# First S5 layer of a four-layer trunk: a written transfer order with the small parameters ahead of x, and the turns and maps of three blocks moved in the instruction order

## Chip, cores and metric

The kernel runs on one core of one Trainium2 chip. The metric is the device time of one execution in microseconds (us), smaller is better. An execution of the kernel before takes 2290.04 us (median of 3 runs, 2288.98 to 2294.23).

The engines are named as the profile names them: PE (TensorE, matmuls), PEld (its weight loads), DVE (VectorE), ACT (ScalarE), POOL (GpSimd), SP (SyncE, which here only issues transfers). A "q" behind the name (SPq) is the engine's sequencer.

## The reference, cut to what matters

Four layers run over a sequence of 512 rows of width 1024, each a mixer and a feed-forward part. Layers 0 and 3 have an S5 mixer, layer 1 a gated linear attention, layer 2 a differential attention. The change is in the S5 mixer of layer 0, which for every group of 16 channels runs a diagonal complex recurrence with 64 states:

```
h = rmsnorm(x, norm_mix[layer])
dt = exp(log_dt)[:, None];  ab_mag = exp(lr * dt);  ab_ang = li * dt
bb = f * b                                # f from ab and lam
p_mag = exp(lr * dt * j);  p_ang = li * dt * j
s[t] = ab * s[t-1] + bb u[t]              # per group, complex
y = Re(c s) + d_skip * h
z = gelu(y);  a, b = split(z @ w_glu, 2);  mix = a * sigmoid(b)
```

## The kernel before

`s5_first` (L1596) computes the S5 mixer of layer 0. The kernel turns the complex recurrence into a real one by rotating with the angle of every state and step: a block of 128 state rows times 512 columns needs the cosine and sine of its angles (tile `cs`), the decay (`r4`), an input operator (`inm`), an output operator (`out`, four parts) and a direct operator, the map (`mop`, from the tile `rps`). Eight blocks, kk = 0 to 7, pass through a pipeline, `s5_pipe` (L1399), one step of its loop for each; operators of two blocks at a time come from the small parameters, in four groups of 8 channel pairs (h = kk // 2).

The steps of one block, with their lines:

- `up` (L1424, copy L1437): PE transposes the scaled input of the block, ACT copies it out.
- `products` (L1445, tile `V`): PE multiplies it with the input operator; the operator is X, made on DVE (L1131, L1106 to L1108), turned on PE (L1247, `xps`), copied by ACT (L1270).
- `states` (L1450 to L1455): six DVE operations multiply V with `cs`.
- `scan` (L1459) and `turn` (L1468, L1472): DVE runs the recurrence and turns the result back (`prods`).
- `outputs` (L1479, L1481, tile `y`): PE multiplies with the map and the output operator; ACT takes the gelu (L1483).
- `turned` (L1493 `zp`, L1494) and `rest` (L1497): PE transposes back, ACT and DVE split the result in a high and a low part.
- `glu` (L396 to L398): products with `w_glu`, whose tiles are split in two by ACT (L368) and DVE (L376).

The angles of a block come in four pieces, `s5_phases_first` (L1054): "rough" (two PE matmuls, L1066 and L1067, into a bank `rough`, then two ACT operations, L1068 and L1070, which round to whole turns, `turnsr`), "angle" (three PE matmuls, L1074 to L1076, of which L1075 subtracts `turnsr`), "clip" (DVE, L1079) and "sines" (ACT, L1082 to L1084). They need a row of frequencies, `frow`, which PE makes in two halves (L1049, copied by ACT at L1050): blocks 0 to 3 and blocks 4 to 7.

The map of a group, `s5_map` (L1216), takes `rps` (PE, L1213, `s5_rows`): DVE adds the skip term (L1223), ACT copies the rest (L1227), then the result goes through DRAM (L1229, L1238) into the map's place.

The small parameters are worked out in `s5_small` (L895): six small transfers (L916 to L923), four PE transposes (L930, L931, tile `s5ps`), then a chain of small DVE operations up to the parts of the frequency rows (L1044) and the first group's X. `loads()` (L1626), called in it behind the six, issues x (L1629, two transfers of 1 MB each), the norm's gain in pieces of 16 numbers (L1632, two transfers) and the raw b and c of the first two groups (L1116, L1119).

What sets the order: the order on an engine is the scheduler's own, except where `hand(...)` (L328) names an engine; from there to the next `hand` that engine's instructions stand as the code is written. In front of the first S5 layer `hand` names PE and ACT; `s5_pipe` then calls `hand_all` (all five engines). Inside the loop of `s5_pipe`, hooks written in `s5_first` (`first`, `behind_states`, `operators`, `ahead_of_zp`, `behind_products`, `behind_scans`, `beside`, `last`) say behind which step the angle pieces, maps and operators are written. An engine works through its instructions in that order: one that waits holds up all behind it.

Of the kernel before, what the change touches and what calls it, by code (L numbers as in the profile page):

```python
# [288 lines left out]
class Trunk:  # L289
# [1306 lines left out]
    def s5_first(self, ctx):  # L1596
# [5 lines left out]
        with self.tc.tile_pool(name="s5_0", bufs=1) as p:  # L1602
            scr, more = (self.hp.tile([P, 4096], F32, tag="hT", name=f"scr{z}") for z in range(2))
            oms = [more[:, 1024 * z : 1024 * z + 1024].rearrange("p (a b) -> p a b", a=2) for z in range(2)]
            mops = [more[:, 2048 + 1024 * z : 3072 + 1024 * z] for z in range(2)]
            bp = p.tile([P, 2, 256], F32, name="bpad")
            rs = p.tile([P, 2, 112], F32, name="rsb")
            self.rows_room = Slices(self.wp.tile([P, 2048], F32, tag="whl", name="params2", bufs=5))
            self.iota = self.rows_room.tile([P, P], I32, name="mi")
            nc.gpsimd.iota(self.iota[:], pattern=[[1, P]], base=0, channel_multiplier=0)  # L1610
            self.hand(mybir.EngineType.PE, mybir.EngineType.Activation)
            for z in range(2):
                self.zero_off(oms[z], 64, one=self.ones[:, :64])
            nc.vector.memset(rs[:, :, :48], 0.0)
# [23 lines left out]
            X, Q, ph, r4 = {}, {}, {}, {}  # L1638

            def new_x(h):  # L1640
                X[h] = self.s5_x(nc.vector, p, 0, 8 * h, 8, raw[h][0], 2, gain)
                X[h][1]()

            def new_q(h):
                Q[h] = self.s5_q(nc.vector, p, 0, 8 * h, 8, 2)
                Q[h][1](self.s5_qt(raw[h][1]))
# [30 lines left out]
            def phases(*pieces):  # L1677
                for kk, name in pieces:
                    if name == "rough":
                        ph[kk] = self.s5_phases_first(kk, cs(kk))  # L1680
                    ph[kk][name]()

            def decays(kk):
                r4[kk] = p.tile([P, 512], F32, tag="r4", name="r4", bufs=2)
                self.s5_decays(0, kk, r4[kk][:])

            def ins(kk):
                self.s5_inms(inm[kk % 2], self.s5_xts(X[kk // 2][0], 4 * (kk % 2)))

            def out_pads(kk):  # L1690
                self.s5_out_pads(oms[kk % 2], Q[kk // 2][0], slice(4 * (kk % 2), 4 * (kk % 2) + 4))
# [18 lines left out]
            def first(kk):  # L1710
                if kk == 2:
                    raw[3] = self.s5_loads(p, 0, 24, 8, 2)
                if 1 <= kk < 7:
                    decays(kk + 1)
                if kk == 2:
                    phases((5, "angle"), (6, "rough"))

            def behind_states(kk):
                if kk == 0:
                    new_x(1)  # L1720
                    X[1][2]()
                if kk == 1:
                    X[1][3]()
                    self.s5_b_pads(bp, X[1][0])
                if kk == 2:
                    phases((6, "angle"), (7, "rough"))

            def operators(kk):
                if kk == 1:
                    phases((3, "angle"), (4, "rough"))  # L1730
                if kk in (2, 4, 6):
                    h = kk // 2
                    self.s5_map(0, 8 * h, 8, self.s5_rows(8, bp, Q[h][0]), rs, mops[h % 2])
                if kk == 1:
                    new_q(1)
                if 1 <= kk < 7:
                    ins(kk + 1)
                if kk in (3, 5):
                    new_q(kk // 2 + 1)

            def ahead_of_zp(kk):
                if kk == 1:
                    phases((4, "angle"), (5, "rough"))
                if kk == 2:
                    phases((7, "angle"))

            def behind_products(kk):
                if kk == 0:
                    phases((2, "angle"))
                    rows[1]()  # L1750
                if kk == 3:
                    phases((5, "sines"), (6, "sines"), (7, "sines"))
                if kk % 2 == 0 and 2 <= kk < 7:
                    out_pads(kk + 1)
# [10 lines left out]
            def beside(kk):  # L1765
                h = kk // 2
                if kk == 0:
                    phases((2, "clip"), (2, "sines"), (3, "rough"))
                if kk == 1:
                    phases((4, "clip"), (3, "sines"), (4, "sines"))  # L1770
                if kk == 2:
                    phases((6, "clip"), (7, "clip"))
                if kk in (2, 4):
                    new_x(h + 1)
                    X[h + 1][2]()
                    X[h + 1][3]()
                    self.s5_b_pads(bp, X[h + 1][0])
                if kk % 2 and kk < 7:
                    Q[h + 1][2]()
                    Q[h + 1][3]()  # L1780
                    if kk > 1:
                        out_pads(kk + 1)

            def last(kk):
# [3 lines left out]
            rv = {}  # L1788
            hooks = {
                "first": first, "operators": operators, "behind states": behind_states, "ahead of zp": ahead_of_zp,  # L1790
                "behind products": behind_products, "behind scans": behind_scans, "beside": beside, "last": last, "late": (1,),
            }
            accs = self.s5_pipe(0, hu, zT, True, room, get, before, hooks)
# [743 lines left out]
```

## Time and profile before

| what | us |
|---|---|
| median of 3 runs (lowest, highest) | 2290.04 (2288.98, 2294.23) |
| the profiled execution's own time | 2288.5 |
| its span, first to last instruction | 2286.7 |
| PE busy | 2203.8 (96% of the span) |
| DVE busy | 1561.3 (68%) |
| ACT busy | 1120.9 (49%) |
| first S5 layer up to the last product of its second glu half | about 0 to 192 |

The profile is one execution, recorded instruction by instruction; all times in it are from the start of its span. 1.8 us of the execution lie outside the span. A row of the timeline has the start, the duration, the engine, the line, the operation and the tiles (out<-in), and in brackets the idle time of the engine before it with what ended that. A row of the chain of waits has start, time and what was on it. A row of the windows view has a stretch, its length, and each engine's busy time in it, then the clock granted to PE (1.00 is full), the busy share of the transfer engines and what they moved. "Queue" rows give the median time from a transfer's issue to its landing.

### The profile page before, as it was taken

How to read it: one execution, taken by the hardware profiler on the slowest of the kernel's cores; microseconds unless marked ns; L12 is line 12 of the kernel's file. 1: busy time of each engine (PE TensorE's matmuls, PEld its weight loads, DVE VectorE, ACT ScalarE, POOL GpSimd, SP SyncE). 2: the span in 40 equal slices, each digit the busy share in tenths (PEclk: the TensorE clock that was granted, in tenths of full speed). 3: DMA queues.
4: the chain of work that ended last, by engine and by line, in shares of the span. 5: the costliest groups of instructions: out<-in, count | busy, mean ns of one | idle time of the engine just before them, and what ended most of it. 6: DMA issues, size and time to landing. Idle time of an engine off the chain costs nothing.

```text
span 2286.7 us, 37220 instructions
## 1 busy us (share of the span) xinstructions
PE 2203.8 (96%) x14847; PEld 1957.1 (86%) x14847; DVE 1561.3 (68%) x2420; ACT 1120.9 (49%) x1870; POOL 281.3 (12%) x392
## 2 busy tenths in 40 slices
PE   4989999999999999999999999999999899999997
PEld 2778979898877799898988887999998788989996
DVE  7783887776624468777754675876766964957674
ACT  5534655454452366555545675744544234635352
POOL 1000141513000011101002131111000100101000
PEclk9899999999999999999999999999999999999999
DMA  3246666664322358666346466885641546767521
GB/s 83 41 113 188 146 170 177 159 177 118 113 75 77 121 135 204 179 172 175 88 139 133 94 147 163 225 217 140 175 101 39 153 142 157 185 165 175 155 77 65
DMA packets 295463, 317.83 MB, mean 139 GB/s; under 512 B 72221, under 2 KB 235353, under 8 KB 294906
## 3 DMA queue, kind: packets, MB, share of 16 engines
q1 hardware_dynamic: 233050, 234.23, 34.0%
q0 software_dynamic: 62240, 81.22, 19.1%
q8 instruction: 117, 1.92, 0.3%
q14 instruction: 56, 0.46, 0.1%
HBM read 283.54 MB, written 16.65 MB: 131 GB/s over the span
## 4 chain that ended last, share of the span: by engine, by line
PE 82%; DVE 8%; ACT 4%; issue 3%; DMA 2%; SPq 1%; POOL 0%; ACTq 0%; DVEq 0%; POOLq 0%
PE a L565 18%; PE acc L396 14%; PE acc L398 13%; PE acc L397 13%; PE c L565 8%; PE d L565 4%; PE y L1481 2%; DVE whl L376 2%; ACT whl L368 1%; PE s L2302 1%; PE V L1445 1%; PE op L2336 1%; PE tp L123 1%; PE y L1479 1%; DVE halves L229 1%
## 5 line engine op out<-in xcount | busy, mean ns | idle before, releaser
L376 DVE TENSOR_TENSOR whl<-wst,whl 128x1024 fp32r<-128x1024 f32 x272 | 331.5, 1224 | 258.0 <-ACT whl L368 257.3
L368 ACT CAST whl<-wst 128x1024 fp32r<-128x1024 f32 x272 | 283.8, 1050 | 307.5 <-PE acc L398 225.3
L565 PE MATMUL a<-side,whl 128*128 128x256 f32 x3168 | 382.5, 277 | 4.0 <-DVE whl L376 3.6
L565 PEld LDWEIGHTS a<-side,whl 128*128 128x128 f32 x3168 | 369.2, 188 | 6.8 <-DVE whl L376 5.4
L396 PE MATMUL acc<-whl,act 128*128 128x512 f32 x704 | 278.4, 396 | 1.7 <-DVE x L548 1.7
L397 PE MATMUL acc<-whl,act 128*128 128x512 f32 x704 | 274.7, 390 | 0.0
L398 PE MATMUL acc<-whl,act 128*128 128x512 f32 x704 | 274.7, 390 | 0.0
L565 PE MATMUL c<-side,whl 128*128 128x256 f32 x2112 | 254.3, 277 | 1.2 <-DVE whl L376 1.2
L565 PEld LDWEIGHTS c<-side,whl 128*128 128x128 f32 x2112 | 246.7, 188 | 2.0 <-DVE whl L376 2.0
L376 DVE TENSOR_TENSOR whl<-slot,whl 128x1024 fp32r<-128x1024 f32 x107 | 130.5, 1223 | 70.0 <-ACT whl L368 70.0
L396 PEld LDWEIGHTS acc<-whl,act 128*128 128x128 f32 x704 | 132.1, 188 | 32.1 <-issue 2.7
L398 PEld LDWEIGHTS acc<-whl,act 128*128 128x128 f32 x704 | 132.2, 188 | 28.1
L397 PEld LDWEIGHTS acc<-whl,act 128*128 128x128 f32 x704 | 132.2, 188 | 25.5
L368 ACT CAST whl<-slot 128x1024 fp32r<-128x1024 f32 x107 | 112.1, 1053 | 82.7 <-PE acc L398 34.9
L396 PE MATMUL acc<-whl,hT 128*128 128x512 f32 x352 | 142.5, 405 | 0.0
L398 PE MATMUL acc<-whl,hT 128*128 128x512 f32 x352 | 137.9, 392 | 0.0
L397 PE MATMUL acc<-whl,hT 128*128 128x512 f32 x352 | 137.8, 391 | 0.0
L565 PE MATMUL a<-sides,whl 128*128 128x256 f32 x1056 | 134.5, 283 | 0.0
L565 PEld LDWEIGHTS a<-sides,whl 128*128 128x128 f32 x1056 | 129.7, 191 | 1.2
L565 PE MATMUL d<-sides,whl 128*128 128x256 f32 x1056 | 126.5, 276 | 1.0 <-ACT whl L368 1.0
L565 PEld LDWEIGHTS d<-sides,whl 128*128 128x128 f32 x1056 | 122.8, 188 | 1.2 <-ACT whl L368 1.2
L704 ACT CAST act<-r 128x512 fp32r<-128x512 f32 (+1 forms) x110 | 66.3, 646 | 115.0 <-DVE r L683 107.8
(458 smaller groups left out, 3879.2 us busy)
## 6 DMA issues: line engine op xcount, KB each, us to landing
wst<-in_ffn_w_gate_up_dram SPq DMA_DIRECT2D x88, 512.0 KB, 4.7
wst<-in_ffn_w_down_dram SPq DMA_DIRECT2D x88, 512.0 KB, 4.3
slot<-in_ffn_w_gate_up_dram SPq DMA_DIRECT2D x71, 512.0 KB, 5.8
wst<-in_ffn_w_gate_up_dram POOLq DMA_DIRECT2D x44, 512.0 KB, 6.2
halves<-in_ffn_w_gate_up_dram SPq DMA_DIRECT2D x43, 512.0 KB, 5.0
wst<-in_s_w_glu_dram SPq DMA_DIRECT2D x32, 512.0 KB, 4.5
wst<-in_gla_w_in_dram SPq DMA_DIRECT2D x24, 512.0 KB, 3.6
wst<-in_diff_w_qkv_dram SPq DMA_DIRECT2D x24, 512.0 KB, 4.2
```

What stands on the lines that cost most here:

```text
L123: tr.nc.tensor.transpose(p[:, j], h[:, j * P : (j + 1) * P], tr.ident[:])
L229: v.tensor_tensor(s, s, y, op=op)
L368: self.last["high"] = self.nc.scalar.copy(hl[:, 0], w[:])
L376: self.last["low"] = self.nc.vector.tensor_tensor(hl[:, 1], w[:], hl[:, 0].bitcast(F32), op=ALU.subtract)
L396: mm(out, lh, rh, start=first, stop=False)
L397: mm(out, lh, rl, start=False, stop=False)
L398: self.last["mm"] = mm(out, ll, rh, start=False, stop=last)
L565: mm(o, hl[:, x, k, c], side[y][:, k], start=first and not (j or k or n), stop=k == 3 and n == 2, skip_group_check=True,)
L704: self.last["act high"] = nc.scalar.copy(dst[:, 0, j], src[:, j])
L1445: mm(V[kk][z][:, bs(b)], inm[:, z, bs(b)], U[:, bs(b)], start=True, stop=True)
L1479: mm(yb[:, b], U[:, bs(b)], mop[:, bs(b)], start=True, stop=False)
L1481: mm(yb[:, b], q[:, j, b], om[:, j // 2, bs(b)], start=False, stop=j == 3)
```

## The change

Three edits, all in `s5_first`; no operation is added or taken away.

1. `hand` names SP too, in front of the small parameters. SP's transfers then stand as written: the six small ones first, x and the gain behind them.
2. The rough turns of the fourth block (kk = 3) are written behind the angle of the third in `behind_products(0)`, ahead of the second half of the frequency rows, where they stood in `beside(0)` behind the sines of block 2.
3. The third step (kk = 2): the map of the second group (`rps` and what takes it) is written in `behind_states`, ahead of block 1's outputs, where it stood in `operators`, behind them; the angle pieces of blocks 5, 6 and 7 each move one or two hooks later.

```
-            self.hand(mybir.EngineType.PE, mybir.EngineType.Activation)
+            self.hand(mybir.EngineType.PE, mybir.EngineType.Activation, mybir.EngineType.SP)
...
             def first(kk):
...
-                if kk == 2:
-                    phases((5, "angle"), (6, "rough"))
+
+            def maps(kk):
+                h = kk // 2
+                self.s5_map(0, 8 * h, 8, self.s5_rows(8, bp, Q[h][0]), rs, mops[h % 2])
...
             def behind_states(kk):
...
                 if kk == 2:
-                    phases((6, "angle"), (7, "rough"))
+                    maps(2)
+                    phases((5, "angle"), (6, "rough"))
...
             def operators(kk):
...
-                if kk in (2, 4, 6):
-                    h = kk // 2
-                    self.s5_map(0, 8 * h, 8, self.s5_rows(8, bp, Q[h][0]), rs, mops[h % 2])
+                if kk in (4, 6):
+                    maps(kk)
...
             def ahead_of_zp(kk):
...
                 if kk == 2:
-                    phases((7, "angle"))
+                    phases((6, "angle"), (7, "rough"))
...
             def behind_products(kk):
                 if kk == 0:
-                    phases((2, "angle"))
+                    phases((2, "angle"), (3, "rough"))
                     rows[1]()
+                if kk == 2:
+                    phases((7, "angle"))
...
             def beside(kk):
...
                 if kk == 0:
-                    phases((2, "clip"), (2, "sines"), (3, "rough"))
+                    phases((2, "clip"), (2, "sines"))
```

How the instructions stand. On SP, from its first transfer on, the kernel before has x (`xin`) and one half of the gain at the head:

```order
L1629 DMA xin<-in_x_dram 128x2048 x2
L1632 DMA gain<-in_norm_mix_dram 64x32x16
L916 DMA params<-in_s_lam_re_dram 64x128
L917 DMA params<-in_s_lam_im_dram 64x128
L919 DMA params<-in_s_log_dt_dram 64x2
L921 DMA params<-in_s_d_dram 16x128
L922 DMA params<-in_norm_mix_dram 8x128
L923 DMA params<-in_norm_ffn_dram 32x128
L1632 DMA gain<-in_norm_mix_dram 64x32x16
L1116 DMA bb<-in_s_b_re_dram 128x8x16
```

The changed kernel, from the same place:

```order
L916 DMA params<-in_s_lam_re_dram 64x128
L917 DMA params<-in_s_lam_im_dram 64x128
L919 DMA params<-in_s_log_dt_dram 64x2
L921 DMA params<-in_s_d_dram 16x128
L922 DMA params<-in_norm_mix_dram 8x128
L923 DMA params<-in_norm_ffn_dram 32x128
L1629 DMA xin<-in_x_dram 128x2048 x2
L1632 DMA gain<-in_norm_mix_dram 64x32x16 x2
L1116 DMA bb<-in_s_b_re_dram 128x8x16
```

The six small transfers have gone past x and the first half of the gain; both halves of the gain now follow each other. Everything behind is in the old order.

On ACT, in the first step of the loop, behind the copy of block 2's input (- is before, + is the changed kernel; `frow` is the second half of the frequency rows, `rsb` the first group's map):

```order
 L1437 COPY room_352<-up 128x512
+L1068 ACTIVATE turns<-rough,magic 128x512
+L1070 ACTIVATE turnsr<-turns,mmagic 128x512
 L1050 CAST frow<-frow 12x512
 L1227 COPY rsb<-rps 128x2x48
```

The two roundings of block 3 stood behind six sine operations (L1082 to L1084, blocks 1 and 2) and now stand ahead of them.

On PE, in the third step, behind the transposes of block 0's result (`zp`), the first rows of the piece that moved (up to the first outputs of block 1):

```order
 L1481 MATMUL y<-scr_97,prods 128x128 x4
 L1493 MATMUL zp<-ident,gain 128x128 x4
-L1074 MATMUL angle<-counts,frow 128x512
-L1075 MATMUL angle<-turnsr,nident 128x512
-L1076 MATMUL angle<-counts,frow 128x512
-L1066 MATMUL rough<-counts,frow 128x512
-L1067 MATMUL rough<-counts,frow 128x512
+L1213 MATMUL rps<-Q,bpad 32x64 x16
 L1074 MATMUL angle<-counts,frow 128x512
 L1075 MATMUL angle<-turnsr,nident 128x512
```

The map's matmuls (`rps`) now stand right behind `zp`; they stood behind the eight rows of block 1's outputs. Block 5's angle stands behind them, block 6's angle behind block 4's `up`, block 7's rough behind that, and block 7's angle behind block 3's products. DVE's order is the same in both kernels.

## Prediction

> **What bounds it now.** I read the chain of waits first, then the timeline of the first 157 us by engine, then the windows view, to see what an earlier S5 layer is worth at the end of the kernel.
>
> The chain's head (start, time, what):
>
> ```profile
> 2.50 5.78 SPq L916
> 8.33 0.60 SPq L917
> 8.97 0.60 SPq L919
> 9.61 0.58 SPq L921
> 10.23 0.37 SPq L922
> 10.65 1.67 DMA params<-in_norm_ffn_dram
> ...
> 12.75 0.49 DVE params L940 x3
> ```
>
> The kernel begins with a queue. The issue of the first small parameter takes 5.78 us, behind the two transfers of x and one of the gain; five more issues follow, the last lands 1.67 us after its issue, and only at 12.75 us can DVE start on the parameters. From there to 27.38 us the chain is DVE's small operations, then PE's frequency rows.
>
> The windows view (length, busy PE, PEld, DVE, ACT, POOL with counts, granted PE clock, transfer share, GB/s):
>
> ```profile
> 51.73:61.97 10.24, 6.83 (x56) 5.18 (x56) 10.21 (x17) 6.76 (x14) 0.10 (x1) 0.50 0.44 88
> 72.21:75.62 3.41, 1.90 (x6) 0.95 (x6) 1.92 (x2) 2.96 (x5) 0.10 (x1) 1.00 0.62 87
> 75.62:82.45 6.83, 6.83 (x28) 6.02 (x28) 0.00 (x0) 1.41 (x2) 0.00 (x0) 0.50 0.09 21
> 91.88:156.57 64.69, 56.78 (x571) 50.77 (x569) 64.21 (x110) 25.28 (x46) 0.31 (x3) 0.97 0.30 64
> 157.00:192.00 35.00, 34.33 (x174) 28.69 (x174) 12.58 (x12) 12.88 (x16) 0.86 (x1) 1.00 0.61 203
> 192.00:2286.70 2094.70, 2056.40 (x13651) 1834.80 (x13649) 1418.60 (x2106) 1029.70 (x1719) 270.59 (x358) 0.99 0.55 143
> ```
>
> From 91.88 to 156.57 DVE is the bound (64.21 of 64.69 us busy); from 157 to the end PE is (34.33 of 35, then 2056.40 of 2094.70). Nothing behind the layer waits for a clock time: its weights are loaded as buffers come free. So every microsecond by which DVE reaches the stretch from 91.88 earlier should come through to the end. The two places that the change touches in the loop lie just ahead, and there PE ran at half clock (0.50) for 10.24 and 6.83 us.
>
> **Edit 1, the transfer order.** Without the queue in front, lam_re's issue should take what its neighbour of the same size, lam_im (L917), takes: 0.60 us, with a step to the next of 0.64 (8.33 to 8.97). The last small one is then issued at 0.81 (SP's first issue) + 3 × 0.64 + 0.62 + 0.42 = 3.77 us instead of 10.65: **6.9 us earlier**. DVE would start at about 5.9. The rows that bear on its cover (the timeline's, and L971 from the chain):
>
> ```profile
> 0.81 0.87 SPq L1629 DMA_DIRECT2D xin<-in_x_dram  x2
> 8.80 1.13 ACT L1386 ACTIVATE scr<-xin,rs 128x1024 f32<-128x1024 f32 x1
> 19.11 0.26 ACT L891 ACTIVATE params<-params 128x64 f32<-128x64 f32 x1 [9.18 <-DVE params L887]
> 21.39 0.27 DVE pw L971
> 25.86 0.42 DVE L1131 TENSOR_TENSOR bb<-bb,gain 128x256 f32<-128x256 f32 x1
> 27.38 1.02 PE L1049 MATMUL frow<-ident,params 128*12 128x128 f32 x4 [14.66 <-DVE params L1044]
> ```
>
> What pays for it is x, which goes out right behind, at about 4.1 instead of 0.81: 3.3 us later. ACT scales the first part of x ahead of the two sines of the parameters, up to 8.80 + 1.13 = 9.9 here, so up to 13.2 at the latest. The first sine would like to start at 19.11 − 6.9 = 12.2; a microsecond late, the two end some 0.7 us behind that, at 13.9, and DVE takes them (L971) at 21.39 − 6.9 = 14.5. Covered, with 0.6 us to spare. DVE and PE have nothing else to do at 5.9.
>
> The other cover is thinner. The gain's second half now stands right behind the first and takes over the stall, and the raw b behind it is wanted at 25.86 − 6.9 = 19.0 (a row of the timeline, and one of the transfers by line, with the median us to landing at its end):
>
> ```profile
> 11.68 1.26 SPq L1116 DMA_DIRECT2D bb<-in_s_b_re_dram  x1
> bb<-in_s_b_im_dram SPq DMA_DIRECT2D x3, 64.0 KB, 2.9
> ```
>
> The stall ended at 2.50 + 5.78 = 8.3, 7.5 us after x's first issue, so now at 11.6. Then comes 1.3 for b's real part, which here took the delay that the second gain makes, and its imaginary part lands 2.9 after its own issue: 15.8, or 17.1 if the second gain costs as much again. That leaves 2 to 3 us of slack; a stall twice as long (5.8 more) would cost DVE 2.6 to 3.9. I take −6.9, with ends −3 and −6.9.
>
> **Edit 2, block 3's turns.** Rows of the timeline:
>
> ```profile
> 54.37 0.72 ACT L1070 ACTIVATE turnsr<-turns,mmagic 128x512 fp32r<-128x512 f32 x1
> 55.14 0.80 PE L1075 MATMUL angle<-turnsr,nident 128*128 128x512 f32 x1 [6.49 <-ACT turnsr L1070]
> 56.39 0.56 DVE L1108 TENSOR_TENSOR X<-X,dx 128x384 f32<-128x384 f32 x1
> 59.34 1.97 PE L1247 MATMUL xps<-ident,X 64*64 64x64 f32 x32
> 63.55 0.69 DVE L1079 TENSOR_SCALAR cs<-angle 128x512 f32<-128x512 f32 x1 [1.39 <-PE angle L1076]
> ```
>
> PE waits 6.49 us for a rounding that ACT does behind six sines. Moved ahead of them it is done five to six us earlier, and that wait goes. But PE's next work but one, the turn of X (`xps`), needs DVE's X, ready at 56.95. In old times it can start at 57.0 instead of 59.34: **2.3 us**, not 6.5; the rest of the wait moves to `xps`. Queued behind `xps` are block 3's `up`, block 4's angle, block 2's products and block 0's outputs, all of which move with it. DVE itself gains only the 1.39 us of its wait at L1079. The price: two roundings of some 0.7 us each stand ahead of the frequency rows, the first map's copy and block 1's sines on ACT, so these come up to 1.4 us later; the sines are wanted by DVE's states of block 1, five operations further on, so I cost it at nothing, and at 0.5 if that cover is short.
>
> The clock moves this term. PE's work from L1075 to `xps` took 59.34 − 55.14 = 4.2 us at half clock; begun some 5.5 us sooner, it ends by about 53.8, and PE is idle for 3 us until 57.0. So a half-clock stretch will be there, shorter or a window longer. `xps` at full clock (1.15 in the next part's rows, against 1.97 here) would make it −3.1; one more 3.41 us stretch at half speed costs 1.7 us of PE and leaves −0.6. I take −2.0.
>
> **Edit 3, the second group's map.**
>
> ```profile
> 71.70 0.50 PE L1074 MATMUL angle<-counts,frow 12*128 12x512 f32 x1
> 73.35 0.39 PE L1074 MATMUL angle<-counts,frow 12*128 12x512 f32 x1
> 73.37 1.23 DVE L376 TENSOR_TENSOR whl<-wst,whl 128x1024 fp32r<-128x1024 f32 x1 [0.25 <-ACT whl L368]
> 75.25 0.50 PE L1075 MATMUL angle<-turnsr,nident 128*128 128x512 f32 x1 [1.51 <-ACT turnsr L1070]
> 77.25 0.80 PE L1479 MATMUL y<-scr,room 128*128 128x128 f32 x2
> 84.38 0.69 PE L1213 MATMUL rps<-Q,bpad 128*32 128x64 f32 x32
> 85.13 1.15 PE L1247 MATMUL xps<-ident,X 64*64 64x64 f32 x32
> 85.17 0.37 DVE L1223 SCALAR_TENSOR_TENSOR rsb<-mask,dcol,rps 128x16 f32<-128x16 f32 x2 [10.58 <-PE rps L1213]
> 90.28 0.48 PE L396 MATMUL acc<-whl,zT 128*128 128x512 f32 x1
> 90.68 1.29 DVE L1079 TENSOR_SCALAR cs<-angle 128x512 f32<-128x512 f32 x2
> ```
>
> This is the longest wait of the layer: DVE stands 10.58 us in front of the map's skip term, and scan, turns and all behind it stand too. Now `rps` follows `zp` and takes 0.75 (84.38 to 85.13), from 71.70 to 72.5, so DVE can go on at 74.6, as soon as L376 ends. Not all of 10.6 us is won, since block 7's angle has gone back behind block 3's products, and DVE's clip of it (the second of the two at 90.68, so 91.3) stands ahead of the next X. PE's way there: `rps` 0.75; block 1's outputs; `xps`, `up`, one angle, `zp` and block 3's products, which ran from 85.13 to 90.28, 5.15; and besides two angles and one rough, of which an angle with a rough took 1.65 (71.70 to 73.35) and an angle alone some 1.2. With the outputs as here, mostly at half clock (77.25 to 84.38, 7.1 us), the sum is 71.70 + 0.75 + 7.13 + 5.15 + 1.65 + 1.2 = 87.6: **−3.7**. At the full clock of block 0's outputs (rows below, 65.80 to 70.46, 4.7 us) it is 85.2: **−6.1**.
>
> ```profile
> 65.80 0.39 PE L1479 MATMUL y<-scr,room 128*128 128x128 f32 x2
> 70.46 0.60 ACT L1483 ACTIVATE gain<-y 128x512 f32<-128x512 f32 x1
> ```
>
> Behind the clip everything is DVE's: X, block 3's states, and its gapless stretch. Does the clock stay up? In the kernel before it fell behind the stretch from 72.21 to 75.62, in which PE was busy 1.90 of 3.41 us, with the 1.51 us wait at L1075 in it. `rps` now fills part of that gap, and block 6's rounding is no longer waited for there. I give it even odds and take the middle, −4.9.
>
> The Trainium skill (TensorE: Matmul & The Clock Gate, section "What's actually happening") says that the clock halves after at least one idle window of about 3.4 us and returns after one busy window. By that rule half-idle windows do no harm, block 1's outputs run at full clock, edit 3 gives its far end, and the whole change 1.2 us more than my sum. The trace disagrees: a window busy 56% was followed by two at half clock, the first of them fully busy.
>
> **Sum.** −6.9 − 2.0 − 4.9 = **−13.8 us**. The profiled execution (2288.5: 2286.7 of span and 1.8 around it) would become 2274.7. The median of the runs shown is 1.5 us above that execution, so I predict **2276.2**. All ends together give −3 − 0.6 + 0.5 − 3.7 = −6.8 and −6.9 − 3.1 − 6.1 = −16.1.
>
> **Rivals.**
>
> *Only the head counts.* PE, idle ahead of `xps`, stays at half clock from there to block 7's angle: the other 9 us of that way (5.15 + 1.65 + 1.2 + 0.75) double too, DVE waits at both clips, and what edits 2 and 3 give is gone. For it: half clock followed both waits of before, and PE has a new one at `xps`. Against: the longest half-clock stretch here was 10.24 us, and it ended while PE was busy. Time: 2290.0 − 6.9 = 2283.1.
>
> *x or b comes late.* The pieces of gain and b are queued behind x, and if the stall doubles, DVE stands at L1131 for up to 3.9 us. For it: the trace shows the stall's size once. Against: the transfer behind the second gain took only 1.26. Time: 2290.0 − 13.8 + 3.9 = 2280.1.
>
> *The small parameters gain nothing.* If the first small transfer is slow whatever stands in front of it, the head stays. Against: x's two issues, the first of all, took 0.87 together. Time: 2290.0 − 2.0 − 4.9 = 2283.1.
>
> *Slower: the clock never comes back.* PE runs DVE's stretch from 91.88 to 156.57 at half clock as well, since DVE-fed work leaves gaps in every window. There PE has 7.9 us of room (64.69 − 56.78), and each 3.41 us stretch at half speed takes 1.7 of it. The first five cost nothing; from about thirteen on the 13.8 us are gone, and with all nineteen the time is 2290.0 − 13.8 + 19 × 1.7 − 7.9 = 2300.6. Against: PE's clock there is 0.97 now, with the same gaps.
>
> **How the numbers follow.** A difference of 0.2% (4.6 us) is about what a measurement of this kernel can tell from no change. Forecast (−9 to −17): 0.72. Only the head: 0.12. x or b late: 0.08, still faster by over 0.2%. Head gains nothing: 0.05, of which I put 0.03 within 0.2%. Slower: 0.03, of which 0.02 beyond 0.2%. Faster by over 0.2%: 0.92, leaving some of the "only the head" cases inside the bound; within: 0.06; slower: 0.02. The range goes from 2271.5 (the far ends, 2290.0 − 16.1 = 2273.9, less 2.4 for the spread of runs, 2288.98 to 2294.23) to 2283.5, which takes in the first three rivals at their own times.
>
> **What would show it.** In the changed kernel's profile: lam_re's issue under 1 us, the stall at a gain transfer, DVE's L940 near 5.9 and PE's L1049 near 20.5. PE's wait at L1075 for block 3's turns gone, and one of 2 to 5 us at `xps` ended by DVE's X. DVE's wait at L1223 gone, and two short ones at L1079 ended by PE's angle. The stretch of DVE at full load starting near 78. I would be wrong if DVE's L1131 waits for a transfer, or if PEclk shows more than five half-clock stretches between 45 and 90 us.

## The result, and the profile after

| | changed kernel | kernel before |
|---|---|---|
| median of 7 runs each, us | 2281.15 (2275.9 to 2285.19) | 2291.11 (2288.98 to 2294.44) |
| the profiled execution's own time | 2281.29 | 2288.5 |
| its span | 2279.4 | 2286.7 |

The ratio is 0.9953, with a 95% interval from 0.9939 to 0.9967: 10.8 us off 2291, between 7.6 and 14.0. The prediction was 13.8 off, 2276.2, with a range from 2271.5 to 2283.5. The two profiled executions are only 7.3 us apart in span; that of before is 2.6 us below its median, that of after at its median.

The head first: the changed kernel's timeline of SP.

```profile
0.81 0.57 SPq L916 DMA_DIRECT2D params<-in_s_lam_re_dram  x1
...
5.04 6.68 SPq L1632 DMA_DIRECT2D gain<-in_norm_mix_dram  x2
```

lam_re's issue, 5.78 us before, takes 0.57; the stall has moved to the gain's two (6.68 together, of which the second took 5.97). Next, DVE's timeline of the changed kernel, from the first parameters to the last clip.

```profile
5.94 0.49 DVE L940 COPY params<-s5ps 128x64 f32<-128x64 f32 x3 [1.63 <-PE s5ps L931]
...
14.79 0.27 DVE L971 TENSOR_TENSOR pw<-params 128x64 f32<-128x64 f32 x1
...
32.73 0.69 DVE L1450 TENSOR_TENSOR mods<-V,cs 128x512 f32<-128x512 f32 x1 [0.64 <-ACT cs L1084]
...
47.17 0.69 DVE L1450 TENSOR_TENSOR mods<-V,cs 128x512 f32<-128x512 f32 x1 [1.19 <-ACT cs L1084]
...
68.33 1.23 DVE L376 TENSOR_TENSOR whl<-wst,whl 128x1024 fp32r<-128x1024 f32 x1 [0.25 <-ACT whl L368]
69.47 0.37 DVE L1223 SCALAR_TENSOR_TENSOR rsb<-mask,dcol,rps 128x16 f32<-128x16 f32 x2
...
76.74 0.69 DVE L1079 TENSOR_SCALAR cs<-angle 128x512 f32<-128x512 f32 x1 [1.68 <-PE angle L1076]
80.85 0.69 DVE L1079 TENSOR_SCALAR cs<-angle 128x512 f32<-128x512 f32 x1 [3.42 <-PE angle L1076]
...
87.03 0.68 DVE L1450 TENSOR_TENSOR mods<-V,cs 128x512 f32<-128x512 f32 x1
```

The same places in DVE's timeline of the kernel before (those that the prediction did not show):

```profile
38.58 0.69 DVE L1450 TENSOR_TENSOR mods<-V,cs 128x512 f32<-128x512 f32 x1 [0.65 <-ACT cs L1084]
...
51.74 0.69 DVE L1450 TENSOR_TENSOR mods<-V,cs 128x512 f32<-128x512 f32 x1
...
97.47 0.68 DVE L1450 TENSOR_TENSOR mods<-V,cs 128x512 f32<-128x512 f32 x1
```

Read the shift down the layer. L940 is 6.8 us earlier (5.94 against 12.75), block 0's states 5.9 (32.73 against 38.58), block 1's 4.6 (47.17 against 51.74), L376 5.0 (68.33 against 73.37), and behind the map and the clips block 3's states 10.4 (87.03 against 97.47). So the head arrives in full and is partly lost by block 1; edit 2 adds nothing that can be seen; edit 3 adds 5.4. The wait of 10.58 us at L1223 is gone and two others, 1.68 and 3.42, stand at L1079. Now PE's timeline of the changed kernel:

```profile
20.79 1.02 PE L1049 MATMUL frow<-ident,params 128*12 128x128 f32 x4 [14.89 <-DVE params L1044]
...
29.91 3.52 PE L1445 MATMUL V<-room,inm 128*128 128x128 f32 x16
...
44.78 0.50 PE L1075 MATMUL angle<-turnsr,nident 128*128 128x512 f32 x1 [0.57 <-ACT turnsr L1070]
...
52.44 1.12 PE L1247 MATMUL xps<-ident,X 64*64 64x64 f32 x16 [3.82 <-DVE X L1108]
...
113.67 0.46 PE L1479 MATMUL y<-scr,room 128*128 128x128 f32 x2 [2.21 <-DMA scr<-rd]
```

L1049 is 6.6 us earlier, L1075 waits 0.57 instead of 6.49, and a wait of 3.82 us for DVE's X stands at `xps`. Two things are not in the prediction. V of block 0 took 3.52 us; before it took 2.05, since PE was back at full clock by then. And the first y of block 5 waits 2.21 us for the map that comes out of DRAM; behind it DVE waits 1.48 us for PE at its last L1223. The chain of waits of the changed kernel runs through that trip:

```profile
105.15 1.83 DMA rd<-rsb
107.38 1.75 SPq L1238
111.54 1.89 DMA scr<-rd
```

Behind 110 us the shift shrinks from 10.4 to 8.0 (the first L376 behind the last scan at 151.17 instead of 159.17). In a second profile of the kernel before that L376 stands at 160.24, so rows this far down are good to about 1 us. That leaves three questions: what took part of the head's gain, what edit 2 is worth, and what the map's trip costs.

### The profile page after: what moved, and what is told of

The parts are those of the page before. It is cut to its first block, busy times and chain, and to the rows that moved or that the text cites. A ratio compares the mean times of both kernels' runs of the same rounds, so it can differ in the third digit from the quotient of the medians.

```text
span 2279.4 us, 37223 instructions
## 1 busy us (share of the span) xinstructions
PE 2204.5 (97%) x14847; PEld 1956.4 (86%) x14847; DVE 1560.5 (68%) x2420; ACT 1120.6 (49%) x1870; POOL 281.6 (12%) x392
## 4 chain that ended last, share of the span: by engine, by line
PE 81%; DVE 9%; ACT 4%; issue 2%; DMA 2%; SPq 1%; POOL 0%; ACTq 0%; DVEq 0%; POOLq 0%
PE a L565 17%; PE acc L396 14%; PE acc L398 13%; PE acc L397 13%; PE c L565 8%; PE d L565 4%; PE y L1481 2%; DVE whl L376 2%; ACT whl L368 1%; PE V L1445 1%; PE s L2306 1%; PE op L2340 1%; PE tp L123 1%; DMA wst<-in_ffn_w_gate_up_dram 1%; DVE halves L229 1%
## 5 line engine op out<-in xcount | busy, mean ns | idle before, releaser
L376 DVE TENSOR_TENSOR whl<-wst,whl 128x1024 fp32r<-128x1024 f32 x272 | 331.6, 1224 | 260.2 <-ACT whl L368 259.4
L376 DVE TENSOR_TENSOR whl<-slot,whl 128x1024 fp32r<-128x1024 f32 x107 | 130.5, 1223 | 70.2 <-ACT whl L368 70.2
```

The costliest lines, as they stand in the source:

```text
L376: self.last["low"] = self.nc.vector.tensor_tensor(hl[:, 1], w[:], hl[:, 0].bitcast(F32), op=ALU.subtract)
```

## The experiments

Each kernel ran beside the kernel before on the same chip; a ratio is to that kernel, with its 95% interval. By these intervals the difference of two rows of the table is uncertain by some 4 us. In the table, us saved is (1 − ratio) × 2291; "block 1" is the start of block 1's L1450 in the profile. "52 products" and the like are extra PE products whose result nobody reads; their place is given with the run.

| run | median us | ratio | us saved | block 1 |
|---|---|---|---|---|
| edit 1 | 2284.95 | 0.9971 [0.9958, 0.9984] | 6.6 | 47.70 |
| edits 1, 2 | 2284.34 | 0.9973 [0.9962, 0.9984] | 6.2 | 48.64 |
| edits 1, 3 | 2279.48 | 0.9956 [0.9944, 0.9969] | 10.1 | 47.43 |
| changed kernel (1, 2, 3) | 2281.15 | 0.9953 [0.9939, 0.9967] | 10.8 | 47.17 |
| 1, 2, 3 + 100 products | 2287.02 | 0.9978 [0.9967, 0.9988] | 5.0 | 52.07 |
| 1, 2, 3 + 52 products | 2277.69 | 0.9936 [0.9923, 0.9949] | 14.7 | 44.91 |
| 1, 3 + 52 products | 2275.42 | 0.9929 [0.9916, 0.9943] | 16.3 | 45.22 |
| before + 52 products | 2288.93 | 0.9994 [0.9984, 1.0003] | 1.4 | 52.10 |
| 1, 2, 3 + 52 + 10 products | 2278.88 | 0.9941 [0.9929, 0.9952] | 13.5 | 45.25 |
| 1, 2, 3, map on two queues | 2278.61 | 0.9939 [0.9926, 0.9951] | 14.0 | 47.33 |
| 1, 2, 3 + 52 + 10, two queues | 2276.07 | 0.9924 [0.9913, 0.9936] | 17.4 | 45.28 |
| the same, turns one step later | 2275.32 | 0.9931 [0.9916, 0.9945] | 15.8 | 43.82 |

### Edit 1 alone

```diff
-            self.hand(mybir.EngineType.PE, mybir.EngineType.Activation)
+            self.hand(mybir.EngineType.PE, mybir.EngineType.Activation, mybir.EngineType.SP)
```

> Edit 1 alone. Theory (each edit is paid at its own place, the turns cost about what they give, the map gives 5 and loses 2.4 of it later): PE's frequency rows L1049 at 20.8 as in the changed kernel, DVE's states of block 0 (L1450) 6 to 6.6 us earlier than before, less where the clock's turn to full falls late; DVE's wait of about 10.6 us at L1223 is back; time 2291.1 less 6 = 2285 (2283.5 to 2287). Rival 'only the head counts': as fast as the changed kernel, 2281 to 2283. The prediction's own sum would have it at 2284.2, with 6.9 of the 13.8.

Measured: 2284.95, 6.6 us saved (3.7 to 9.6), beside 6.9 in the prediction's sum. DVE's timeline of this run:

```profile
47.70 0.69 DVE L1450 TENSOR_TENSOR mods<-V,cs 128x512 f32<-128x512 f32 x1 [1.66 <-ACT cs L1084]
...
68.60 1.23 DVE L376 TENSOR_TENSOR whl<-wst,whl 128x1024 fp32r<-128x1024 f32 x1 [0.25 <-ACT whl L368]
...
80.27 0.37 DVE L1223 SCALAR_TENSOR_TENSOR rsb<-mask,dcol,rps 128x16 f32<-128x16 f32 x2 [10.44 <-PE rps L1213]
...
92.55 0.68 DVE L1450 TENSOR_TENSOR mods<-V,cs 128x512 f32<-128x512 f32 x1
```

The long wait at L1223 is back, so the head is not all that counts. But block 1's L1450 waits 1.66 us for ScalarE's sine, and no rounding of edit 2 stands in front of that sine here.

### Edits 1 and 2

```diff
-                    phases((2, "angle"))
+                    phases((2, "angle"), (3, "rough"))
...
-                    phases((2, "clip"), (2, "sines"), (3, "rough"))
+                    phases((2, "clip"), (2, "sines"))
```

> Edits 1 and 2 without 3. Theory (block 3's roundings on ScalarE delay block 1's sines, and DVE pays it): DVE waits about 1.2 us at block 1's L1450 for ScalarE's sine L1084, PE's wait at L1075 is under 1 us, the wait at xps for DVE's X is 3 to 5 us, and DVE reaches L1223 no earlier than in the run with edit 1 alone; time within 1 us of that run. Rival (the prediction's term): 2.0 us faster than edit 1 alone.

Measured: 2284.34, 6.2 us saved (3.7 to 8.7): the same as edit 1 alone. DVE's timeline:

```profile
48.64 0.69 DVE L1450 TENSOR_TENSOR mods<-V,cs 128x512 f32<-128x512 f32 x1 [2.61 <-ACT cs L1084]
...
70.22 1.23 DVE L376 TENSOR_TENSOR whl<-wst,whl 128x1024 fp32r<-128x1024 f32 x1 [0.26 <-ACT whl L368]
```

In these two profiles PE came back to full clock at nearly the same time (near 39 us, by its rows), so they can be set side by side. The wait at block 1's L1450 grows by 0.95 us, L1079 no longer waits (0.64 with edit 1 alone), and L376 is no earlier (70.22 against 68.60). Block 3's states start 1.8 us later (94.36 against 92.55).

### Edits 1 and 3

```diff
-                    phases((2, "angle"), (3, "rough"))
+                    phases((2, "angle"))
...
-                    phases((2, "clip"), (2, "sines"))
+                    phases((2, "clip"), (2, "sines"), (3, "rough"))
```

(against the changed kernel)

> Edits 1 and 3 without 2. Theory: block 1's L1450 does not wait for a sine and starts near 45.9, PE waits 5 to 6.5 us at L1075 for block 3's rounding, xps does not wait for X; DVE has no long wait at L1223; time within 1.5 us of the changed kernel, on either side (2279.5 to 2282.5). Rival (the prediction's term for edit 2): 2.0 us slower than the changed kernel, 2283. Against edit 1 alone, edit 3 by itself gives 4 to 5 us.

Measured: 2279.48, 10.1 us saved (7.1 to 12.8), the same as the changed kernel's 10.8. DVE's timeline:

```profile
47.43 0.69 DVE L1450 TENSOR_TENSOR mods<-V,cs 128x512 f32<-128x512 f32 x1 [1.42 <-ACT cs L1084]
...
68.19 1.23 DVE L376 TENSOR_TENSOR whl<-wst,whl 128x1024 fp32r<-128x1024 f32 x1 [0.25 <-ACT whl L368]
...
86.89 0.68 DVE L1450 TENSOR_TENSOR mods<-V,cs 128x512 f32<-128x512 f32 x1
```

From L376 to block 3's L1450 it is 23.95 us with edit 1 alone and 18.70 here: edit 3 is worth 5.25 at its place. With edit 2 in both kernels it is 24.14 (70.22 to 94.36) and 18.70 (68.33 to 87.03): 5.4. On one point my theory fell: without edit 2, block 1 should not have waited for a sine, and it waits 1.42. Something else delays that sine, and what these runs share is a PE at half clock up to 39 us.

### 100 products ahead of the frequency rows

```diff
             self.s5_small(p, loads, lambda: next(inputs))
+            warm = self.sbank("warm")
+            for n in range(100):
+                nc.tensor.matmul(warm[:, :P], self.ident[:], self.ident[:], start=True, stop=True)
```

> The changed kernel with 100 extra PE products of the identity by itself (into a bank that is not read) behind the turn of the small parameters, ahead of the frequency rows: they keep PE busy from about 5.9 to 19 us. Theory (the head's gain is partly eaten by PE's half clock between 20.8 and 33 us): granted clock 1.0 from about 13 us on, V of block 0 takes 2.0 us instead of 3.5 and starts 1.5 to 3 us earlier, DVE's L1450 of block 0 at 30 to 31.5 instead of 32.7; time 1 to 3 us below the changed kernel. Rival (DVE and ScalarE set the pace there, the clock is beside the point): L1450 of block 0 within 0.5 us of 32.7 and no change in time.

Measured: 2287.02, 5.0 us saved; slower than the changed kernel. The number was far too high. PE's timeline of this run:

```profile
5.62 25.23 PE L1640 MATMUL warm<-ident 128*128 128x128 f32 x200
30.68 0.60 PE L1049 MATMUL frow<-ident,params 128*12 128x128 f32 x4
```

and DVE's:

```profile
38.90 0.69 DVE L1450 TENSOR_TENSOR mods<-V,cs 128x512 f32<-128x512 f32 x1 [0.65 <-ACT cs L1084]
...
52.07 0.68 DVE L1450 TENSOR_TENSOR mods<-V,cs 128x512 f32<-128x512 f32 x1
```

A product is two instructions here, and 200 of them held the frequency rows back by 9.9 us. What the run shows all the same, with PE at full clock from L1049 on (V of blocks 0 and 1 in 2.05 and 1.95 us): from L1049 to block 0's L1450 it is 8.2 us at full clock (30.68 to 38.90), 11.9 in the changed kernel (20.79 to 32.73), though some of DVE's own work was done while it waited. And block 1's L1450 follows block 0's after 13.17 us without a wait, edit 2's roundings included; before it was 13.16, in the changed kernel 14.44.

### 52 products

> The changed kernel with 52 extra PE products of the identity by itself (into a bank that is not read) ahead of the frequency rows; the 100 of the run before took 25.23 us, of which by their rates some 6 us at half clock, so 52 end between 18 and 20.5 us and delay nothing. Theory (PE's half clock in the head eats the gain): DVE's L1450 of block 0 at 30.7 (32.73 in the changed kernel), that of block 1 at about 43.9 without a wait for the sine (47.17 there): 2 to 3.3 us earlier; PE's half clock ahead of 40 us is gone; time about 2278, 2 to 3.5 us below the changed kernel's 2281. Rival (edit 2's roundings on ScalarE cost DVE 1.2 us whatever the clock): L1450 of block 1 still waits over 1 us for L1084. Second rival (later waits take it back): time as the changed kernel's.

The same edit with `range(52)`. Measured: 2277.69, 14.7 us saved (11.7 to 17.6), against the changed kernel's 10.8. PE's timeline:

```profile
5.70 13.99 PE L1640 MATMUL warm<-ident 128*128 128x128 f32 x104
...
27.79 3.39 PE L1445 MATMUL V<-room,inm 128*128 128x128 f32 x16
```

and DVE's:

```profile
30.70 0.69 DVE L1450 TENSOR_TENSOR mods<-V,cs 128x512 f32<-128x512 f32 x1 [0.65 <-ACT cs L1084]
...
44.91 0.69 DVE L1450 TENSOR_TENSOR mods<-V,cs 128x512 f32<-128x512 f32 x1 [0.98 <-ACT cs L1084]
```

Block 0's states start at 30.70, as expected, 2.0 us earlier than without the products, and block 1's 2.3 us earlier. The clock was not full throughout, as I had wanted it: it fell again for V of block 0 (3.39 us), and with it a wait of 0.98 us at block 1 stays. By block 3 the gain is gone from the rows: its states start at 87.92, against 87.03 in the changed kernel, with V of block 2 wholly at half clock (3.78 us). At the first L376 behind the last scan this run is 1.5 us ahead again (149.68 against 151.17), since DVE's wait at its last L1223 is gone. So the 3.9 us of the time, themselves inside the uncertainty, cannot be traced to the head alone.

### 52 products in the kernel before

> The kernel before (none of the three edits) with the same 52 extra PE products ahead of its frequency rows. Theory (the clock's return took part of edit 1's gain: it came 7.3 us after the frequency rows began in the kernel before, and 12 to 19 us after it in the profiled runs with edit 1): before has less to win from a warm PE; DVE's L1450 of block 0 at 36.5 instead of 38.58 (PE's rows end earlier, DVE's own work then sets it), that of block 1 2.1 us earlier too, since it did not wait before; time 0 to 2 us below the kernel before, against 3.9 that the changed kernel won. Rival (the clock is a constant cost of both, and took nothing of the gain): before wins as much as the changed kernel did, 3.5 to 4 us.

Measured: 2288.93, a ratio of 0.9994 whose interval holds 1: 1.4 us saved, at most 3.7. DVE's timeline:

```profile
37.29 0.69 DVE L1450 TENSOR_TENSOR mods<-V,cs 128x512 f32<-128x512 f32 x1 [0.65 <-ACT cs L1084]
...
52.10 0.69 DVE L1450 TENSOR_TENSOR mods<-V,cs 128x512 f32<-128x512 f32 x1 [1.57 <-ACT cs L1084]
```

Block 0 gains 1.3 us and block 1 nothing (52.10 against 51.74), where 2.1 us had been expected. The reason stands in PE's timeline:

```profile
34.47 1.86 PE L1445 MATMUL V<-room,inm 128*128 128x128 f32 x7
35.69 2.55 PE L1445 MATMUL V<-room,inm 128*128 128x128 f32 x11
```

V of block 0 took 3.77 us (34.47 to 38.24), for 2.05 without the products: the clock fell behind them, and PE's rows come back to their full-clock lengths only near 44 us. So this run is no clean test of whether the kernel before has less to win from a warm PE, and the two gains in time, 3.9 and 1.4, have intervals that overlap. What it does show is a kernel without any of the three edits that waits 1.57 us for block 1's sine once V of block 0 runs at half clock.

### The kernel before once more

> The kernel before, word for word, profiled once more: when does PE's clock come back in the head? If it is the program that sets it, at 34 to 35 us again, with V of block 0 in 2.05 us; if it is chance, anywhere from 34 to 46, with V of block 0 at up to 3.8 us and DVE's L1450 of block 1 up to 2 us later.

Measured: 2289.31 in its one run, and the head repeats to 0.04 us. PE's timeline of this second profile, with two rows from the end of the layer:

```profile
34.87 0.49 PE L1075 MATMUL angle<-turnsr,nident 128*128 128x512 f32 x1
...
35.72 2.05 PE L1445 MATMUL V<-room,inm 128*128 128x128 f32 x16
...
124.28 0.46 PE L1479 MATMUL y<-scr,room 128*128 128x128 f32 x2 [0.84 <-DMA scr<-rd]
...
152.53 0.46 PE L1479 MATMUL y<-scr,room 128*128 128x128 f32 x2 [2.32 <-DMA scr<-Q]
```

The last two are the first y of blocks 5 and 7: the kernel before also waits there, at block 5 for a transfer of its map, at block 7, by the profile, for the one that SP issues right behind the map's eight (in its first profile 0 and 1.99 us). The clock returns near 34.7, 7.3 us after L1049's start, in both profiles of the kernel before. With edit 1 alone:

```profile
38.80 0.79 PE L1074 MATMUL angle<-counts,frow 12*128 12x512 f32 x1
39.52 0.50 PE L1075 MATMUL angle<-turnsr,nident 128*128 128x512 f32 x1
```

it returns near 39.5, 18.7 us after. In the five profiles with edit 1 and no extra products (edit 1; 1, 2; 1, 3; 1, 2, 3; two queues) it took 12 to 19 us.

### 52 products without edit 2

> Edits 1 and 3 with the 52 products, without edit 2. Theory (edit 2 is worth nothing: what it saves at L1079 and xps it pays at block 1's sines): time within 1.5 us of the run with all three edits and the 52 products, 2277.7; DVE's L1450 of block 1 no later than 44.0, PE's L1075 waits about 5 us again. Rival (edit 2 pays once PE is warm in the head): 2 us slower, 2280.

Measured: 2275.42, 16.3 us saved (13.1 to 19.2), 1.6 more than with edit 2 and inside the intervals. Against edits 1 and 3 without the products (10.1) it is 6.2 more, clear of the uncertainty; in the rows the products bring 2.2 us at block 1, 1.1 at block 3 and 3.6 at the first L376 behind the last scan (147.00 against 150.56). Block 1's L1450 does not wait, but it starts at 45.22, since block 0's V fell into half clock in this run too; L1079 of block 4 waits 1.62 for PE's angle, where edit 2 has no wait.

### 10 more products ahead of `xps`

```diff
+                if kk == 1:
+                    idle = self.acc("idle")
+                    for n in range(10):
+                        nc.tensor.matmul(idle[:, :P], self.ident[:], self.ident[:], start=True, stop=True)
                 if 1 <= kk < 7:
                     ins(kk + 1)
```

> As the run with 52 products, and 10 more ahead of the turn of X (xps) of block 2, where PE waits 3.8 us for DVE's X in the changed kernel. Theory (a wait at xps is followed by half clock, so moving the wait there gained nothing): the second half of xps, up, angle and V(2) run at full clock (V 2.0 us instead of 3.4), the first y is 2 to 3 us earlier against the start of xps's second half (8.3 us in the changed kernel, 5.5 in the kernel before); together with the head's products 4 to 6 us below the changed kernel, 2275 to 2277. Rival (10 products do not keep the clock up, or the path from xps to y is DVE's): as the run with 52 alone.

Measured: 2278.88, 13.5 us saved (11.0 to 16.3): no better than 52 alone. PE's timeline:

```profile
50.53 0.68 PE L1247 MATMUL xps<-ident,X 64*64 64x64 f32 x16 [0.57 <-DVE X L1108]
...
53.48 2.05 PE L1445 MATMUL V<-room,inm 128*128 128x128 f32 x16
55.36 0.39 PE L1479 MATMUL y<-scr,room 128*128 128x128 f32 x2
```

At its place the theory held: from `xps`'s second half to the first y it is 4.8 us, 8.3 in the changed kernel. But the first L376 behind the last scan is then 3.4 us ahead of the run with 52 products (146.24 against 149.68), and the two spans are equal (2276.7 and 2276.5): in this profile the clock also fell in the stretches from 1300 to 1400 and from 1700 to 1800 us more than there (0.98 and 0.95 of full against 1.00 and 0.97). Whether a gain in the layer is regularly lost later, or was in this one run, stays open.

### The map's transfers on two queues

```diff
-                self.dq.dma_start(dv[r0 : r0 + 16, :, g], src)
+                (self.nc.gpsimd if g else self.dq).dma_start(dv[r0 : r0 + 16, :, g], src)
```

> The changed kernel with the eight transfers of each map out of DRAM (L1238) given half to SP's queue and half to GpSimd's. Theory (with the layer earlier, the third map's trip through DRAM, 8.5 us from DVE's L1223 to the first y of block 5, ends last: eight issues in a row on SP take 5 of it): PE's wait of 2.2 us at that y is gone or under 0.7, DVE's wait of 1.5 us at the last L1223 is gone, time 1.5 to 3 us below the changed kernel, 2278 to 2279.5. Rival (the clock or PE's own work sets that place; or GpSimd's issues are no faster): wait at y and time unchanged.

Measured: 2278.61, 14.0 us saved (11.2 to 17.0), 3.2 more than the changed kernel, with overlapping intervals. PE's timeline:

```profile
112.26 0.46 PE L1479 MATMUL y<-scr,room 128*128 128x128 f32 x2 [0.62 <-DMA scr<-rd]
...
139.89 0.46 PE L1479 MATMUL y<-scr,room 128*128 128x128 f32 x2 [0.66 <-DMA scr<-rd]
```

The waits of 2.2 us at y of blocks 5 and 7 shrink to 0.6, DVE's last L1223 does not wait, y of block 7 starts 3.6 us earlier (139.89 against 143.46), and the first L376 behind the last scan 3.2 (147.96 against 151.17).

### All three additions

> The three additions together: 52 products in the head, 10 ahead of xps, the map's transfers on two queues. Theory: the gains add, 6 to 8 us below the changed kernel, 2273 to 2275. Rival (each only moves the wait): no more than the best of the three alone.

Measured: 2276.07, 17.4 us saved (14.7 to 19.9). This is the fastest by ratio, and faster than both the changed kernel and the kernel before: the interval, 0.9913 to 0.9936, lies below the changed kernel's. By the ratios it is 6.6 us below the changed kernel, inside the 6 to 8 that was expected; the median is above 2273 to 2275, but the kernel before was at 2292.42 in this batch, not at 2291.11. The two queues are worth 3.9 of it by the ratios and 3.4 at the first L376 behind the last scan (142.80 against 146.24 with the products alone). Whether the kernel before would gain as much from two queues was not run.

### The turns one step later

```diff
-                    phases((2, "angle"), (3, "rough"))
+                    phases((2, "angle"))
...
-                    phases((1, "clip"), (1, "sines"))
+                    phases((1, "clip"), (1, "sines"), (3, "rough"))
```

(against the run with all three additions)

> The fastest run so far (52 products, 10 products, the map on two queues) with block 3's rough turns one step later: behind block 1's sines and ahead of block 2's, instead of ahead of both. Theory (edit 2's price is the 1.4 us for which DVE waits at block 1's L1450): that wait is gone, L1450 of block 1 at 43.9 instead of 45.28, L1075 waits some 1.5 us and nothing behind it moves; 1.0 to 1.5 us below that run, 2274.5 to 2275. Rival (the wait only moves on to xps or L1079): the same time.

Measured: 2275.32, a ratio of 0.9931: no gain. DVE's timeline:

```profile
43.82 0.69 DVE L1450 TENSOR_TENSOR mods<-V,cs 128x512 f32<-128x512 f32 x1
...
55.59 0.69 DVE L1079 TENSOR_SCALAR cs<-angle 128x512 f32<-128x512 f32 x1 [1.34 <-PE angle L1076]
...
60.06 0.68 DVE L1450 TENSOR_TENSOR mods<-V,cs 128x512 f32<-128x512 f32 x1
...
84.11 0.68 DVE L1450 TENSOR_TENSOR mods<-V,cs 128x512 f32<-128x512 f32 x1
```

The wait at block 1 is gone as expected (43.82 against 45.28), and it comes back, 1.34 us long, at L1079: block 2's states start at 60.06, against 60.09 in the run before. The rival was right: block 1's sines and block 3's turns want the same stretch of ScalarE, and DVE pays for either. Behind that the earlier turns are ahead: block 3's states start at 84.11 here, at 82.44 in the run before, where PE turned X 2.0 us earlier (`xps` at 50.55 instead of 52.55) with its clock kept up.

## Why the prediction came out as it did

**Edit 1, the head: right.** Every row named came out: L940 at 5.94 (5.9 predicted), L1049 at 20.79 (20.5), the stall on a gain transfer. So did the cover: ScalarE's two sines end at 13.6 and DVE comes to L971 at 14.79 without a wait (14.5 predicted), and L1131 takes b at 19.29 without a wait (19.0). By the times the edit alone is worth 6.6 us (3.7 to 9.6), for −6.9. That x or b would come late did not happen.

**What the head's sum left out: the clock.** I carried the 6.9 us through the head as if PE's rates there were those of before. In the profiles they were not: before, PE was at full clock by V of block 0; with edit 1, V took 3.5 to 3.8 us and the second frequency rows and block 1's sines came late with it. Block 0's states gained 5.9, block 1's only 3.1 to 4.6 of it (48.64 with edits 1 and 2, 47.70 with edit 1, 47.43 with 1 and 3, 47.17 in the changed kernel, against 51.74). At block 1 the runs show that the clock does this: with 100 products, PE at full clock from L1049 on, block 1 follows block 0 after 13.17 us without a wait, as in the kernel before (13.16), and the kernel before itself gets a wait of 1.57 us there once V of its block 0 runs at half clock. What this costs in time is less sure: 52 products bring the changed kernel 3.9 us and edits 1 and 3 6.2, each uncertain by some 4, and in the first of these the rows have lost the gain by block 3. Why the clock needs 12 to 19 us to come back in the one kernel and 7.3 in the other, with the same instructions at the same distances from L1049, is open.

The Trainium skill (TensorE: Matmul & The Clock Gate, section "What's actually happening") says that the clock comes back after one busy window of about 3.4 us. The traces disagree: the changed kernel's PE was busy for all of 20.80 to 33.00 us, by the row below, and V began at half speed 9.1 us into that.

Two rows of the windows view of the changed kernel (stretch, length, busy PE, PEld, DVE, ACT, POOL, granted clock, transfer share, GB/s):

```profile
20.80:33.00 12.20, 12.20 (x75) 8.88 (x76) 9.25 (x20) 6.54 (x10) 0.00 (x0) 1.00 0.16 23
...
46.68:60.33 13.65, 9.83 (x64) 7.24 (x61) 13.10 (x21) 9.36 (x19) 0.10 (x1) 0.50 0.35 69
```

**Edit 2: wrong size, 0 instead of −2.0.** The mechanism was there: L1075's wait fell from 6.49 to 0.57, `xps` waited 3.82 for X. But three pairs of kernels with and without the edit differ by +0.4, −0.7 and +1.6 us (1, 2 against 1; 1, 2, 3 against 1, 3; the same with 52 products). Each difference is uncertain by some 4 us, their mean of +0.4 by some 2.4, so the times alone put −2.0 at the edge; the rows say where it went. The step that failed is the price, "so I cost it at nothing, and at 0.5 if that cover is short". The cover, DVE's five operations ahead of block 1's states, holds at full clock (13.17 us from block 0 to block 1 with the roundings in place) and not at half: with edit 1 alone it is already used up, and the roundings then add 0.95. Where the clock is back by 31 to 33 us it takes both: with the 52 products DVE waits 0.98 with the roundings there and not at all without them. So part of what block 1 loses in the changed kernel is edit 2's own price.

What the edit saves, 0.5 to 1.6 at L1079, pays for that and no more: in all three pairs block 3's states start later with it, by 1.8, 0.1 and 2.1 us. The 2.3 us that `xps` was to gain go, as far as the rows tell, in the 13.65 us of half clock around it: from its second half to the first y it is 8.3 us, 4.8 with the 10 products. That fits the runs with all three additions, where the 10 products keep PE at full clock there and the turns ahead of both blocks' sines, not between them, are 1.7 us ahead at block 3; in the times this is not clear of the uncertainty.

**Edit 3: right.** −4.9 was forecast, with ends −3.7 and −6.1; 5.25 and 5.4 were measured at the place, 3.5 and 4.6 in the times of the pairs. Block 1's outputs ran at full clock (4.7 us, 69.02 to 73.68), the condition of the far end; PE's way from `rps` to the last clip took 14.2 us (66.65 to 80.85), 0.7 more than that sum, so it came out between the middle and the far end. DVE's full load starts at 80.85, not near 78, because the head and edit 2 had brought 5.0 us by L376 and not 8.9.

**Behind the clips: not all DVE's.** The sentence "Behind the clip everything is DVE's" left out the third and fourth map. From DVE's L1223 to the first y of block 5 it is 8.6 us before (114.86 to 123.42, no wait, since PE came late with V at half clock) and 9.2 in the changed kernel (104.44 to 113.67), where PE stands 2.2 us. But the wait is not new: the second profile of the kernel before has 0.84 at that place, and at y of block 7 its two profiles wait 1.99 and 2.32, at the end of the same row of issues, the changed kernel 2.22. So the trip is a cost that the sum left alone in both kernels; how much of the loss from 10.4 to 8.0 is its doing is not shown. With the maps on two queues the waits shrink, and 3.2 us go with them by the ratios and at the end of the layer. Whether the one profiled loss at L1223 (1.48) is regular is not settled: with edits 1 and 3, y waits 1.62 and DVE does not wait, for want of a half-clock stretch behind it.

So of −13.8 the parts are about −6.6, 0 and −4 by the times, and −10.8 was measured together. The total alone could not tell these from the forecast, since 13.8 lies inside its interval of 7.6 to 14.0; that edit 2 gave nothing is read from the pairs and the rows. Of the rivals, "only the head counts" falls with edit 3: 5.25 and 5.4 us in the rows, and 3.5 and 4.6 in the times, whose mean of 4.1 is uncertain by some 3. That PE idle ahead of `xps` stays at half clock was right as far as it went, for 13.65 us, and it ended ahead of block 1's outputs. Between 45 and 90 us those are four half-clock stretches of 3.41 us, inside the five that the prediction allowed. In DVE's long stretch of the changed kernel the clock fell in one window (114.94 to 118.36); the slower rival did not come up.

## What to carry to other kernels

A shift that is worked out at one place is worth what the next engine lets through: carry it from row to row, and ask at each whether the rates of before still hold there, the clock's above all. A wait that is moved off a chain of two engines that take turns (here ScalarE's sines and roundings in front of DVE) comes back at the next hand-over unless work leaves that engine. And a path through DRAM that takes about as long as the work beside it shows in one profile as a wait and in the next not (0 and 0.84 us at the same matmul of the same kernel); look for the rows that arrive with no wait but no slack either.

## What the runs showed of the hardware

- PE can be at half speed while the granted clock reads 1.00: in the row of 20.80 to 33.00 it is 1.00, and V in it took 3.52 us for 2.05. Up to the first change that the records hold, the clock is read from the durations.
- From a standstill the clock came back after some 2 to 4 us of 128 by 128 products (estimated: 200 of them took 25.23 us, 104 took 13.69 to 14.71 us; at the 1.95 us that 16 take in V at full clock it would be 24.4 and 12.7, and each us at half clock adds half a us), and after 7 to 19 us of the layer's own mix, PE busy in both.
- A PE that is 72% busy can stay at half clock: 9.83 of 13.65 us, from 46.68 to 60.33.
- The stall of some 6 us sits behind the first piece of the gain in both orders: 5.78 us on lam_re before, 5.97 on the second piece of the gain after.
- For the third map, four issues take 2.09 us on GpSimd beside 3.1 on SP (from 107.18 us); eight on SP alone take 4.97 (from 107.00).
